# Attention: block mask carried as rows of the second rotary product

## The chip, the cores and the metric

The kernel runs on one core of one Trainium2 chip. The metric is the device time of one execution in microseconds (us); the median of three runs of the kernel before is 1014.16 us (1014.09 to 1014.38).

## What is computed

One residual block of a streaming encoder over 512 frames of width 1024: a half-step SwiGLU layer (ffn1), a token mixer, and a second half-step SwiGLU layer (ffn2), each behind an RMSNorm that is scaled and shifted by vectors computed from a condition c. The mixer has two groups of four heads: a gated DeltaNet, which needs the inverse of a triangular matrix per chunk of 64 frames, and a multi-head latent attention. The change lies in the scores of the attention:

```python
def _rope(x, cos, sin):
    x1, x2 = jnp.split(x, 2, axis=-1)
    return jnp.concatenate([x1 * cos - x2 * sin, x2 * cos + x1 * sin], axis=-1)
...
CHUNK = 64
Q_BLOCK = 128
MLA_NOPE = 128
MLA_ROPE = 64
```

A score is the product of a query and a key over 192 channels: 128 without position ("nope") and 64 rotated by `_rope`; the rotated key is shared by the four heads. The mask is causal by chunks of 64 frames: a query sees every key of its own chunk and of earlier ones. In a block of 128 queries only one corner is masked, the first 64 queries against the last 64 keys of the same block.

## The kernel before, in words

**Stages.** ffn1 runs to about 350 us (the sums for the modulation vectors, L828 on VectorE, run in the same time), the mixer from about 350 to 610 us, ffn2 to the end. Nearly all of TensorE's work is dense products against streamed weights: in the mixer the projection `w_in`, each 128x512 tile as three products of high and low parts (L475, L476, L477). Weights come through tiles `wr` (loaded by SyncE's queue, L139), are cast on ScalarE to `wh` (L234), and VectorE subtracts for the low part `wl` (L235).

**The order.** The mixer's parts are generators: one stream of dense products, and beside it the DeltaNet and the attention in small steps. A scheduler then fixes one order of instructions per engine, so each engine's order is set before the program runs and may change wherever an instruction is added or removed. Every transfer that the steps below name goes through the one queue of SyncE, in order.

**The attention.** `turn_q` (L2070) transposes the rotated queries of two heads at a time; of each head 64 partitions of the tile `qrT` (its own side) take the high part (ScalarE, L2086) and the other 64 the low part (VectorE, L2088). `prep_k` (L2097) transposes the rotated key (`kro`, which holds it twice), and splits it (L2124, with VectorE's subtraction at L1440) into `krh` and `krl`, each holding the key's high or low part on both halves of the partitions. `attend` (L2143) computes the scores of one block of queries and one head, 16 times in all: the nope product in full precision (two passes, L2155), `krh` and `krl` against `qrT` (L2157), and a product of 64 columns in bf16 that adds -1e30 to the masked corner (L2158, from the constant `am` of L1372 to L1376). VectorE takes the maximum (L2160, L2162), ScalarE the exponential (L207), TensorE transposes the result (L2169), ScalarE copies it as `pT` (L2171), and TensorE multiplies it by the values (L2175).

**The inverse.** `delta_a` (L1715) multiplies the DeltaNet keys of each head with themselves (L1712), VectorE scales the result to the tile `at` (L1444), and 16 transfers write it to `a_d` in DRAM. `base_blocks` (L1735) loads it as `ba` (L1746) and VectorE inverts small blocks in a recursion of 15 steps, each a product `bw` (L1444) and a sum `bt` (L1760), which depend on one another; the result goes through DRAM (`t_d`, L1764) to the tile `t` (L1766). `inverse` (L1782) scales it (L1444), multiplies it with `at` in 32x32 tiles (L1806), and goes on from VectorE's `Y` with L1815 and later levels (L1841, L1853, L1877).

Of the kernel before, what the change touches and what calls it, by code (L numbers as in the profile page):

```python
# [11 lines left out]
F32 = mybir.dt.float32  # L12
F32R = mybir.dt.float32r
BF16 = mybir.dt.bfloat16
I32 = mybir.dt.int32
AF = mybir.ActivationFunctionType
ALU = mybir.AluOpType
AX = mybir.AxisListType

P = 128  # L20
NT = 512
D = 1024
KT = D // P
NB = NT // P
# [75 lines left out]
class Block:  # L100
# [1246 lines left out]
    def masks(self):  # L1347
        nc = self.nc
        tile = self.slot(s="mk")
        room = iter([tile[:, i * P:(i + 1) * P] for i in range(4)])  # L1350
        g = nc.gpsimd
        half = next(room).bitcast(BF16)
        self.eye, self.emask = half[:, :P], half[:, P:]
        nc.vector.tensor_copy(self.eye, self.ident)
        g.memset(self.emask, 0.0)
        g.affine_select(out=self.emask, in_=self.emask, pattern=[[1, P]], compare_op=ALU.is_ge, fill=-1.0e30, base=0,
                        channel_multiplier=-1)
        self.triu = next(room)
        g.affine_select(out=self.triu, in_=self.ones, pattern=[[1, P]], compare_op=ALU.is_ge, fill=0.0, base=0,
                        channel_multiplier=-1)  # L1360
        room = next(room)
        by16, self.halves, self.quads, self.lmask = room[:, :8], room[:, 8:10], room[:, 12:16], room[:, 32:64]
        g.affine_select(out=by16, in_=self.ones[:, :8], pattern=[[-16, 8]], compare_op=ALU.is_ge, fill=0.0, base=0,
                        channel_multiplier=1)
        g.affine_select(out=by16, in_=by16, pattern=[[16, 8]], compare_op=ALU.is_ge, fill=0.0, base=15,
                        channel_multiplier=-1)
        nc.vector.tensor_reduce(out=self.halves, in_=by16.rearrange("p (j e) -> p e j", e=2), axis=AX.X, op=ALU.add)
        nc.vector.tensor_reduce(out=self.quads, in_=by16.rearrange("p (j e) -> p j e", e=2), axis=AX.X, op=ALU.add)
        g.memset(self.lmask[:, 16:], 0.0)
        nc.vector.tensor_copy(self.lmask[:, :16], self.halves[:, 1:2].to_broadcast([P, 16]))  # L1370

        am = self.const([P, 192], BF16, s="am")  # L1372
        g.memset(am, 0.0)
        g.memset(am[0:1, 0:64], 1.0)
        g.memset(am[0:1, 128:192], -1.0e30)
        self.amask = am[:, :P], am[:, P:]  # L1376
        sel = self.slot(F32R, s="sel")
        g.memset(sel.bitcast(F32), 0.0)
        self.sel = sel.rearrange("p (h c) -> p h c", h=4)
        for o in (0, 32):  # L1380
            nc.vector.tensor_copy(self.sel[o:o + 4], self.ident[o:o + 4, o:o + 4].unsqueeze(2).to_broadcast([4, 4, P]))
# [692 lines left out]
    def turn_q(self, q):  # L2074

        nc = self.nc
        qr = self.qr
        for g in range(2):
            pt = self.aux()
            for b in range(NB):  # L2080
                nc.tensor.transpose(pt[:, b * P:(b + 1) * P], qr[b][:, g * P:(g + 1) * P], self.ident)

            sides = (slice(0, 64), slice(64, P))
            ts = [self.slot(F32R, "qrT") for _ in sides]
            for t, own in zip(ts, sides):
                nc.scalar.copy(t[own, :], pt[own, :])  # L2086
            for t, own, other in zip(ts, sides, sides[::-1]):
                nc.vector.tensor_tensor(out=t[other, :], in0=pt[own, :], in1=t[own, :].bitcast(F32), op=ALU.subtract)  # L2088
            self.qrT += ts
            yield  # L2090
        for h in range(4):
            c = (h % 2) * 192
            self.qnT.append(self.head_tiles([q[b][h // 2][:, c:c + P] for b in range(NB)], self.gqn))
            yield

    def prep_k(self, kn, q):

        nc = self.nc
        kr = self.kab[:, :288].rearrange("p (b c) -> p b c", b=NB)[:, :, :64]
        s = self.slot(s="krq")  # L2100
# [20 lines left out]
        pt = self.aux()  # L2121
        for b in range(NB):
            nc.tensor.transpose(pt[:, b * P:(b + 1) * P], ko[:, b * P:(b + 1) * P], self.ident)
        self.krT = self.split(pt, "kr")  # L2124
        jk = self.vcol["qkn_k_nope"]
        for h in range(4):
            self.knT.append(self.head_tiles([kn[b][:, h * P:(h + 1) * P] for b in range(NB)], self.cwT[:, jk:jk + 1]))
# [15 lines left out]
    def attend(self, i, h, v, late):  # L2143


        nc = self.nc
# [6 lines left out]
            self.al[h] = self.const([P, NB], s="al")  # L2153
        ps = self.aux()
        nc.tensor.matmul(ps[:, :n], self.qnT[h][:, ts], self.knT[h][:, :n], start=True, stop=False)  # L2155
        for e, kr in enumerate(self.krT):
            nc.tensor.matmul(ps[:, :n], self.qrT[h][:, ts], kr[:, :n], start=False, stop=False)  # L2157
        nc.tensor.matmul(ps[:, n - 64:n], *self.amask, start=False, stop=True)  # L2158
        m = self.small(1, "mx")
        nc.vector.tensor_reduce(out=m, in_=ps[:, :n], axis=AX.X, op=ALU.max, negate=True)  # L2160
        rq = self.rqn[:, 4 * i + h:4 * i + h + 1]
# [44 lines left out]
    def mixer(self, norms):  # L2206
        nc, tc = self.nc, self.tc
        lat = self.latents(norms)
        self.dp = self.ctx.enter_context(tc.tile_pool(name="dp", bufs=1, space=bass.MemoryType.DRAM))
        sides = chain, deltas, att = Side(), Side(), Side()  # L2210
        self.q = self.kv = None
        chain.add(self.lifts(*lat))
# [19 lines left out]
        self.S = None  # L2232

        def prepared():
            self.qrT, self.qnT, self.knT = [], [], []
            while self.q is None:
                yield
            yield from self.prep_q(self.q)
# [250 lines left out]
```

## Time and profile before

| what | value |
|---|---|
| median of three runs | 1014.16 us |
| the profiled execution | 1014.94 us, its span 1013.2 us |
| TensorE (PE) busy | 1001.6 us, 99% of the span |
| VectorE (DVE), ScalarE (ACT) | 822.0 us (81%), 526.7 us (52%) |
| mean granted clock of TensorE | 0.999 of full speed |
| chain that ended last | PE 86%, DVE 7%, DMA 3% |

The span is the time from the first to the last instruction on the core. A busy engine is one that has an instruction in flight; TensorE's products overlap, so the distance from one product's start to the next one's start says what a product takes, and its own duration does not. PEld is TensorE's loading of the stationary operand, which overlaps the products.

### The profile page before, as it was taken

The numbers are of one execution on the slowest core, as the hardware profiler recorded it, in microseconds if no ns is written. First come the engines' busy times: TensorE is split into PE (matmuls) and PEld (weight loads), VectorE is DVE, ScalarE is ACT, GpSimd is POOL, SyncE is SP. The second block draws the span as 40 slices with busy tenths as digits, with TensorE's granted clock in tenths as the row PEclk, the third lists the DMA queues.
The fourth block names the chain that finished last, engine by engine and source line by source line (L and its number), as shares of the span: only waits on it lengthen the run. The fifth ranks groups of instructions, "written<-read, shape, count | busy, mean of one in ns | idle before, by whom it ended". The sixth has DMA issues, their size and how long they took to land.

```text
span 1013.2 us, 18034 instructions
## 1 busy us (share of the span) xinstructions
PE 1001.6 (99%) x7101; PEld 908.1 (90%) x7101; DVE 822.0 (81%) x1461; ACT 526.7 (52%) x954; POOL 30.6 (3%) x74
## 2 busy tenths in 40 slices
PE   7999999999999999999999999999999999999998
PEld 5788999999887889888888888999999999989898
DVE  4779999887797747788987649789998998799984
ACT  4455555556422225548766455375555555655453
POOL 0000000000200000100001012000000000000000
PEclk9999999999999999999999999999999999999999
DMA  9963564434598825412132121212544443323332
GB/s 318 294 203 104 164 209 134 120 97 128 152 324 277 297 78 151 117 44 62 46 75 54 43 63 42 84 43 76 174 122 150 122 129 105 110 83 91 113 104 63
DMA packets 204034, 130.84 MB, mean 129 GB/s; under 512 B 14497, under 2 KB 188590, under 8 KB 203950
## 3 DMA queue, kind: packets, MB, share of 16 engines
q1 hardware_dynamic: 203950, 129.70, 42.0%
q8 instruction: 55, 0.90, 0.4%
q14 instruction: 29, 0.24, 0.1%
HBM read 127.18 MB, written 2.49 MB: 128 GB/s over the span
## 4 chain that ended last, share of the span: by engine, by line
PE 86%; DVE 7%; DMA 3%; issue 1%; SPq 1%; ACT 1%; POOL 0%; DVEq 0%; ACTq 0%
PE pa L360 17%; PE pa L475 13%; PE pb L360 13%; PE pa L476 12%; PE pa L477 12%; PE pa L1207 4%; DMA ar<-in_w_ada 3%; PE pb L1207 3%; SPq L139 1%; PE pb L2175 1%; PE pb L475 1%; PE pb L477 1%; PE pb L476 1%; PE pb L2155 1%; PE pb L1712 1%
## 5 line engine op out<-in xcount | busy, mean ns | idle before, releaser
L275 DVE TENSOR_TENSOR wl<-wr,wh 128x1024 fp32r<-128x1024 f32 x120 | 145.7, 1219 | 26.4 <-ACT wh L279 25.6
L279 ACT CAST wh<-wr 128x1024 fp32r<-128x1024 f32 x120 | 123.2, 1051 | 35.8 <-DVE wr L275 22.0
L234 ACT CAST wh<-wr 128x1024 fp32r<-128x1024 f32 (+1 forms) x77 | 76.8, 1007 | 117.6 <-PE pa L476 106.2
L475 PE MATMUL pa<-hh,wh 128*128 128x512 f32 (+1 forms) x309 | 119.5, 387 | 0.0
L235 DVE TENSOR_TENSOR wl<-wr,wh 128x1024 fp32r<-128x1024 f32 (+1 forms) x77 | 89.2, 1164 | 34.2 <-ACT wh L234 34.1
L477 PE MATMUL pa<-hh,wl 128*128 128x512 f32 (+1 forms) x309 | 116.3, 376 | 0.0
L476 PE MATMUL pa<-hl,wh 128*128 128x512 f32 (+1 forms) x309 | 116.1, 376 | 0.0
L475 PE MATMUL pa<-ah,wh 128*128 128x512 f32 (+1 forms) x262 | 97.9, 374 | 0.0
L476 PE MATMUL pa<-al,wh 128*128 128x512 f32 (+1 forms) x262 | 97.5, 372 | 0.0
L477 PE MATMUL pa<-ah,wl 128*128 128x512 f32 (+1 forms) x262 | 97.3, 371 | 0.0
L275 DVE TENSOR_TENSOR wr<-wr,wr 128x512 f32<-128x512 f32 x120 | 82.4, 687 | 1.7
L828 DVE SCALAR_TENSOR_TENSOR aa<-ar,sc,aa 128x512 f32<-128x512 f32 x98 | 73.3, 748 | 7.7 <-DMA ar<-in_w_ada 6.1
L360 PE MATMUL pa<-th,wh 128*128 128x256 f32 x264 | 74.8, 283 | 0.5 <-ACT z L365 0.5
L360 PE MATMUL pa<-hh,wh 128*128 128x256 f32 x264 | 74.8, 283 | 0.0
L360 PE MATMUL pa<-th,wl 128*128 128x256 f32 x264 | 74.7, 283 | 0.0
L360 PE MATMUL pa<-tl,wh 128*128 128x256 f32 x264 | 74.7, 283 | 0.0
L360 PE MATMUL pa<-hl,wh 128*128 128x256 f32 x264 | 74.7, 283 | 0.0
L360 PE MATMUL pa<-hh,wl 128*128 128x256 f32 x264 | 74.7, 283 | 0.0
L475 PEld LDWEIGHTS pa<-hh,wh 128*128 128x128 f32 x309 | 58.4, 189 | 11.0 <-issue 2.5
L477 PEld LDWEIGHTS pa<-hh,wl 128*128 128x128 f32 x309 | 58.2, 188 | 10.2
L476 PEld LDWEIGHTS pa<-hl,wh 128*128 128x128 f32 x309 | 58.4, 189 | 8.4
L475 PEld LDWEIGHTS pa<-ah,wh 128*128 128x128 f32 x262 | 49.3, 188 | 10.2 <-ACT wh L234 1.7
(484 smaller groups left out, 2768.1 us busy)
## 6 DMA issues: line engine op xcount, KB each, us to landing
wr<-in_ffn_w_in SPq DMA_DIRECT2D x79, 512.0 KB
ar<-in_w_ada SPq DMA_DIRECT2D x128, 256.0 KB
wr<-in_ffn_w_out SPq DMA_DIRECT2D x32, 512.0 KB
wr<-in_w_in SPq DMA_DIRECT2D x21, 512.0 KB
wr<-in_ffn_w_out SPq DMA_DIRECT2D x16, 384.0 KB
wr<-in_w_out SPq DMA_DIRECT2D x8, 512.0 KB
wr<-in_ffn_w_in SPq DMA_DIRECT2D x8, 384.0 KB
ar<-in_w_ada SPq DMA_DIRECT2D x6, 512.0 KB
```

The costliest lines, as they stand in the source:

```text
L139: return self.nc.sync.dma_start(dst, src)
L234: self.nc.scalar.copy(hi, raw)
L235: self.nc.vector.tensor_tensor(out=lo, in0=raw, in1=hi.bitcast(F32), op=ALU.subtract)
L275: sub = lambda out, x, y: nc.vector.tensor_tensor(out=out, in0=x, in1=y, op=ALU.subtract)
L279: nc.scalar.copy(hi[:, :n], raw[:, :n])
L360: nc.tensor.matmul(z, a[:, j, :], b, start=start and j == 0 and i == 0, stop=j == 3 and i == 2, skip_group_check=not start)
L475: mm(out, wh, xh, start=start, stop=False)
L476: mm(out, wh, xl, start=False, stop=False)
L477: mm(out, wl, xh, start=False, stop=stop)
L828: nc.vector.scalar_tensor_tensor(out=acc, in0=a, scalar=sc, in1=acc, op0=ALU.mult, op1=ALU.add)
L1207: nc.tensor.matmul(z, a[:, j, :], b, start=start and j == 0 and i == 0, stop=j == 3 and i == 2, skip_group_check=not start)
L1712: nc.tensor.matmul(pa[:, ps], kh[:, ps], x[:, ps], start=True, stop=True)
```

## The change

`masks` no longer makes the bf16 constant `am`. It makes two tiles of 64 rows and 512 columns: in one (`qm`) row b is 1 over the first half of the columns of block b, in the other (`km`) row b is -1e30 over the second half. Both are written to DRAM. `turn_q` builds a second query tile per head, `qrm`: its own side is a copy of the high part in `qrT`, the other side holds `qm`. `prep_k` builds a tile `krm` for the even heads (low part of the key on the lower half, `km` on the upper), and overwrites the lower half of `krl` with `km` for the odd heads. All these fills are transfers: 2 to DRAM, 8 for the four `qrm`, 3 for `krm` and `krl`. In `attend` the second rotary product takes `krm` or `krl` against `qrm`: it gives the low part of the key times the high part of the query, plus the mask. The product L2158 and its weight load are gone, 16 times. The product of the two low parts, which was part of the score before, is no longer computed.

```diff
--- before.py
+++ after.py
@@ -1369,11 +1369,21 @@
         g.memset(self.lmask[:, 16:], 0.0)
         nc.vector.tensor_copy(self.lmask[:, :16], self.halves[:, 1:2].to_broadcast([P, 16]))
 
-        am = self.const([P, 192], BF16, s="am")
-        g.memset(am, 0.0)
-        g.memset(am[0:1, 0:64], 1.0)
-        g.memset(am[0:1, 128:192], -1.0e30)
-        self.amask = am[:, :P], am[:, P:]
+        self.dp = self.ctx.enter_context(self.tc.tile_pool(name="dp", bufs=1, space=bass.MemoryType.DRAM))
+        one = self.slot(s="am")[:64]
+        g.memset(one, 0.0)
+        by = lambda t: t.rearrange("p (b c) -> p b c", b=NB)
+        first, second = by(one)[:, :, :64], by(one)[:, :, 64:]
+        nc.vector.tensor_copy(first, self.ident[:64, :NB].unsqueeze(2).to_broadcast([64, NB, 64]))
+        qm, km = self.slot(F32R, "am")[:64], self.slot(F32R, "am")[:64]
+        nc.vector.tensor_copy(qm, one)
+        nc.vector.tensor_scalar(out=by(km)[:, :, 64:], in0=first, scalar1=-1.0e30, scalar2=None, op0=ALU.mult)
+        nc.vector.tensor_copy(by(km)[:, :, :64], second)
+        self.amask = []
+        for m in (qm, km):
+            kept = self.dp.tile([64, NT], F32, tag=self.name("am"), name=self.name("am"))
+            self.load(kept, m.bitcast(F32))
+            self.amask.append(kept)
         sel = self.slot(F32R, s="sel")
         g.memset(sel.bitcast(F32), 0.0)
         self.sel = sel.rearrange("p (h c) -> p h c", h=4)
@@ -2087,6 +2097,11 @@
             for t, own, other in zip(ts, sides, sides[::-1]):
                 nc.vector.tensor_tensor(out=t[other, :], in0=pt[own, :], in1=t[own, :].bitcast(F32), op=ALU.subtract)
             self.qrT += ts
+            for t, own, other in zip(ts, sides, sides[::-1]):
+                both = self.slot(F32R, "qrm")
+                self.load(both[other, :].bitcast(F32), self.amask[0])
+                self.load(both[own, :].bitcast(F32), t[own, :].bitcast(F32))
+                self.qrM.append(both)
             yield
         for h in range(4):
             c = (h % 2) * 192
@@ -2121,7 +2136,12 @@
         pt = self.aux()
         for b in range(NB):
             nc.tensor.transpose(pt[:, b * P:(b + 1) * P], ko[:, b * P:(b + 1) * P], self.ident)
-        self.krT = self.split(pt, "kr")
+        self.krT, low = self.split(pt, "kr")
+        even = self.slot(F32R, "krm")
+        self.load(even[64:].bitcast(F32), self.amask[1])
+        self.load(even[:64].bitcast(F32), low[64:].bitcast(F32))
+        self.load(low[:64].bitcast(F32), self.amask[1])
+        self.krM = even, low
         jk = self.vcol["qkn_k_nope"]
         for h in range(4):
             self.knT.append(self.head_tiles([kn[b][:, h * P:(h + 1) * P] for b in range(NB)], self.cwT[:, jk:jk + 1]))
@@ -2153,9 +2173,8 @@
             self.al[h] = self.const([P, NB], s="al")
         ps = self.aux()
         nc.tensor.matmul(ps[:, :n], self.qnT[h][:, ts], self.knT[h][:, :n], start=True, stop=False)
-        for e, kr in enumerate(self.krT):
-            nc.tensor.matmul(ps[:, :n], self.qrT[h][:, ts], kr[:, :n], start=False, stop=False)
-        nc.tensor.matmul(ps[:, n - 64:n], *self.amask, start=False, stop=True)
+        nc.tensor.matmul(ps[:, :n], self.qrT[h][:, ts], self.krT[:, :n], start=False, stop=False)
+        nc.tensor.matmul(ps[:, :n], self.qrM[h][:, ts], self.krM[h % 2][:, :n], start=False, stop=True)
         m = self.small(1, "mx")
         nc.vector.tensor_reduce(out=m, in_=ps[:, :n], axis=AX.X, op=ALU.max, negate=True)
         rq = self.rqn[:, 4 * i + h:4 * i + h + 1]
@@ -2206,7 +2225,6 @@
     def mixer(self, norms):
         nc, tc = self.nc, self.tc
         lat = self.latents(norms)
-        self.dp = self.ctx.enter_context(tc.tile_pool(name="dp", bufs=1, space=bass.MemoryType.DRAM))
         sides = chain, deltas, att = Side(), Side(), Side()
         self.q = self.kv = None
         chain.add(self.lifts(*lat))
@@ -2232,7 +2250,7 @@
         self.S = None
 
         def prepared():
-            self.qrT, self.qnT, self.knT = [], [], []
+            self.qrT, self.qrM, self.qnT, self.knT = [], [], [], []
             while self.q is None:
                 yield
             yield from self.prep_q(self.q)
```

The scheduler's order changes with it. Three places are shown; lines from L1372 on stand 10 to 19 lines further down in the changed code.

**TensorE, ahead of the DeltaNet's key products (L1712, now L1722).** First before, then with the change; `kro` is the rotated key, `kn` are the nope keys, and L475 to L477 on `pa` are dense products.

```order
L1639 MATMUL pb_5371<-rw_5008,sel_3146 128x512
L1640 LDWEIGHTS mk_3129
L1640 MATMUL pb_5371<-mk_3129 128x512
L2123 MATMUL pb_5380<-ident_85,kro_5191 128x128 x4
L2028 MATMUL pb_5389<-ident_85,kn_4900 128x128
```

```order
L1649 MATMUL pb_5391<-rw_5016,sel_3156 128x512
L1650 LDWEIGHTS mk_3129
L1650 MATMUL pb_5391<-mk_3129 128x512
L477 MATMUL pa_5623<-hh_4090,wl_5536 128x512
L475 MATMUL pa_5698<-hh_4076,wh_5619 128x512
L476 MATMUL pa_5698<-hl_4077,wh_5619 128x512
L477 MATMUL pa_5698<-hh_4076,wl_5620 128x512
L475 MATMUL pa_5698<-hh_4078,wh_5619 128x512
L476 MATMUL pa_5698<-hl_4079,wh_5619 128x512
L2138 MATMUL pb_5400<-ident_85,kro_5199 128x128 x4
L477 MATMUL pa_5698<-hh_4078,wl_5620 128x512
L2038 MATMUL pb_5413<-ident_85,kn_4908 128x128
```

Dense products stand ahead of the key's transposes that stood behind them. Counted over the program, 18 more dense products lie ahead of the transposes of `kro`, and 22 more ahead of the last of the 16 key products (L475 to L477 counted alike); two scores lie ahead of it in both orders.

**VectorE, in the last steps of the recursion (L1760, now L1770).** First before, then with the change; `wl` and `cv` are the dense stream's low part and the DeltaNet's convolution.

```order
L1760 TENSOR_REDUCE bt_5618<-bw_5621 128x13
L235 TENSOR_TENSOR wl_6197<-wr_6194,wh_6196 128x1024
L1444 TENSOR_TENSOR bw_5621<-ba_5615,bt_5618 128x196
L1656 SCALAR_TENSOR_TENSOR cv_5853<-pa_5777,cwT_3774,cv_5853 128x511
L1760 TENSOR_REDUCE bt_5618<-bw_5621 128x14
L1656 SCALAR_TENSOR_TENSOR cv_5853<-pa_5777,cwT_3774,cv_5853 128x510
L1444 TENSOR_TENSOR bw_5621<-ba_5615,bt_5618 128x225
L1656 SCALAR_TENSOR_TENSOR cv_5853<-pa_5777,cwT_3774,cv_5853 128x509
L1760 TENSOR_REDUCE bt_5618<-bw_5621 128x15
```

```order
L1770 TENSOR_REDUCE bt_5640<-bw_5643 128x13
L1454 TENSOR_TENSOR bw_5643<-ba_5637,bt_5640 128x196
L1770 TENSOR_REDUCE bt_5640<-bw_5643 128x14
L1454 TENSOR_TENSOR bw_5643<-ba_5637,bt_5640 128x225
L1770 TENSOR_REDUCE bt_5640<-bw_5643 128x15
L235 TENSOR_TENSOR wl_6406<-wr_6403,wh_6405 128x1024
L1666 SCALAR_TENSOR_TENSOR cv_5950<-pa_5882,cwT_3784,cv_5950 128x511
```

Other work that stood between the steps stands behind the last one. Over all 15 steps the recursion has one L235 and three L1656 fewer between its instructions, and one L2160 with its L2162 more; three more of its instructions follow one another with nothing between.

**TensorE, between the 32x32 products of the inverse (L1806 and L1815, now L1816 and L1825).** The rows up to the second of the two, first before, then with the change; `pr` is the exponential of a score.

```order
L2175 MATMUL pb_6055<-vn_4905,pT_5931 128x128
L2169 MATMUL pb_6059<-ident_85,pr_5893 128x128 x3
L475 MATMUL pa_5948<-hh_4074,wh_5860 128x512
L476 MATMUL pa_5948<-hl_4075,wh_5860 128x512
L477 MATMUL pa_5948<-hh_4074,wl_5861 128x512
L475 MATMUL pa_5948<-hh_4076,wh_5860 128x512
L476 MATMUL pa_5948<-hl_4077,wh_5860 128x512
L477 MATMUL pa_5948<-hh_4076,wl_5861 128x512
L1815 MATMUL pb_6071<-T_5918,Y_6020 32x32 x64
```

```order
L2194 MATMUL pb_6071<-vn_4913,pT_5948 128x128
L2188 MATMUL pb_6075<-ident_85,pr_5910 128x128 x3
L1825 MATMUL pb_6087<-T_5935,Y_6037 32x32 x64
L477 MATMUL pa_5965<-hh_4090,wl_5879 128x512
```

The six dense products between L1806 and L1815 are gone from there: 11 more stand ahead of L1806, 5 more ahead of L1815. Seven scores lie ahead of L1806 in both orders.

SyncE's queue changes at one place that matters beside these. Before, one load of `w_in`, 8 of the 16 dumps of `at`, another load of `w_in` and the other 8 dumps follow one another. With the change the 8 fills of `qrm`, a load of `w_in`, one of `w_out`, and the 3 fills of `krm` and `krl` stand ahead of all 16 dumps.

## Rows read from the trace of the kernel before

**Rows 1.** The page, part 1: busy time, share of the span, instructions.

```profile
PE 1001.6 (99%) x7101; PEld 908.1 (90%) x7101; DVE 822.0 (81%) x1461; ACT 526.7 (52%) x954; POOL 30.6 (3%) x74
```

**Rows 2.** Stretches of 20 us: busy us (count) per engine, clock, DMA share, GB/s.

```profile
540.00:560.00 20.00, 19.54 (x417) 16.27 (x417) 15.36 (x28) 14.69 (x33) 3.53 (x3) 1.00 0.20 57
```

**Rows 3.** Timeline of PE: start us, duration us, line; two dense products 16 apart.

```profile
507.73 0.39 PE L475 MATMUL pa<-hh,wh 128*128 128x512 f32 x1
...
511.39 0.39 PE L476 MATMUL pa<-hl,wh 128*128 128x512 f32 x1
```

**Rows 4.** Timeline of PE: end of a score, its mask, the next products.

```profile
587.00 0.40 PE L2157 MATMUL pb<-krl,qrT 128*128 128x512 f32 x1
587.24 0.20 PE L2158 MATMUL pb<-am 128*128 128x64 bf16 x1
587.28 0.48 PE L475 MATMUL pa<-hh,wh 128*128 128x512 f32 x1
587.59 0.39 PE L476 MATMUL pa<-hl,wh 128*128 128x512 f32 x1
```

**Rows 5.** Timeline of PEld, the same place: the weight loads behind the mask's.

```profile
587.24 0.20 PEld L475 LDWEIGHTS pa<-hh,wh 128*128 128x128 f32 x1
587.36 0.19 PEld L476 LDWEIGHTS pa<-hl,wh 128*128 128x128 f32 x1
```

**Rows 6.** Timeline of DVE: the split key, `at`, the recursion, the loaded `t`.

```profile
500.48 0.69 DVE L1440 TENSOR_TENSOR krl<-pb,krh 128x512 fp32r<-128x512 f32 x1
...
509.17 0.69 DVE L1444 TENSOR_TENSOR at<-pb,ed 128x512 f32<-128x512 f32 x1
...
525.50 0.42 DVE L2160 TENSOR_REDUCE mx<-pb 128x1 f32<-128x256 f32 x1
...
526.88 0.22 DVE L1760 TENSOR_REDUCE bt<-bw 128x8 f32<-128x64 f32 x1
527.14 0.30 DVE L1444 TENSOR_TENSOR bw<-ba,bt 128x81 f32<-128x81 f32 x1
...
530.66 1.22 DVE L235 TENSOR_TENSOR wl<-wr,wh 128x1024 fp32r<-128x1024 f32 x1
531.80 0.49 DVE L1444 TENSOR_TENSOR bw<-ba,bt 128x196 f32<-128x196 f32 x1
532.21 0.74 DVE L1656 SCALAR_TENSOR_TENSOR cv<-pa,cwT,cv 128x511 f32<-128x511 f32 x1
...
534.90 0.38 DVE L1760 TENSOR_REDUCE bt<-bw 128x15 f32<-128x225 f32 x1
...
540.82 0.69 DVE L1444 TENSOR_TENSOR t<-t,mk 128x512 f32<-128x512 f32 x1 [0.45 <-DMA t<-t_d]
```

**Rows 7.** Timeline of PE: first score, and around L1806 and L1815.

```profile
503.42 0.28 PE L2157 MATMUL pb<-krl,qrT 128*128 128x128 f32 x1
...
541.28 0.40 PE L477 MATMUL pa<-hh,wl 128*128 128x512 f32 x1
541.65 1.28 PE L1806 MATMUL pb<-t,at 32*32 32x32 f32 x128
...
545.25 0.49 PE L2169 MATMUL pb<-ident,pr 128*128 128x128 f32 x3
...
546.73 0.39 PE L477 MATMUL pa<-hh,wl 128*128 128x512 f32 x1
547.04 1.29 PE L1815 MATMUL pb<-T,Y 32*32 32x32 f32 x128
...
549.43 0.94 PE L2175 MATMUL pb<-vn,pT 128*128 128x128 f32 x6 [0.47 <-ACT pT L2171]
```

**Rows 8.** Timeline of SyncE's queue: the last eight dumps, the load of `t`.

```profile
508.50 3.63 SPq L139 DMA_DIRECT2D a_d<-at  x8
...
538.02 0.37 SPq L1766 DMA_DIRECT2D t<-t_d  x1
```

**Rows 9.** Waits of SyncE's queue from 486 to 545 us: total, times, longest.

```profile
SPq L139 <- DVE wl L235: 31.4, 6, 11.1
```

## The prediction

> **What bounds the kernel.** I read the busy shares first: TensorE is busy 99% of the span [rows 1], so time leaves where TensorE has less to do, and comes where it must wait. The stretches of 20 us come next: nearly all are full, and the one from 540 to 560 us, where the attention runs beside the inverse of the DeltaNet, shows 19.54 of 20 us at a clock of 1.00 [rows 2]. The timeline of TensorE says what stands there. A dense product costs 0.229 us, start to start: 16 steps in 3.66 us [rows 3]. Before the first 32x32 product, L1806, 0.37 us pass from the dense product ahead, where 0.31 pass ahead of L1815, which is not late [rows 7]: so L1806 waits 0.06 us for the tile `t` and stands at the edge. Whatever makes `t` later than TensorE's own place in its work becomes idle time. That is the second thing to look at, beside the products saved.
>
> **The mask products, minus 2.0 us.** Two starts are misleading: the mask's product and the next one are drawn 0.04 us apart. But the second product behind the mask starts 0.59 us after the second rotary product [rows 4], where two dense steps take 0.46 [rows 3]: 0.13 for the mask. The weight loads say why: the load of the product behind the mask begins when the mask's product does, and the load after that begins 0.12 later [rows 5], as that product starts. 64 columns are too short to cover a weight load. So 0.125 times 16 scores is 2.0 us; bounds 16 times 0.04 = 0.6 and 16 times 0.13 = 2.1. I take 2.0, since the weight loads and the distances agree. [...]
>
> **The dense products that move.** The last key product of the DeltaNet comes 22 dense products later and two masks earlier: 22 times 0.229 less 0.25 is +4.8 us [rows 3]. VectorE makes the last `at` 509.17 us in [rows 6]; it follows the second score and the key products behind it, so it moves with them by 4.8. Then comes the chain of dumps, load, recursion, `t_d` and `t`. Its transfers stay as they are. In the recursion one L235 (1.14 from its start to the next) and three L1656 (0.66 each) leave, 3.1 us in all, and a maximum of 0.42 with its small product, some 0.45 together, joins [rows 6]. Three steps more stand bare: a bare one leaves 0.04 us before the next (526.88 plus 0.22, then 527.14), where a covered one overlaps by some 0.08 (530.66 plus 1.22, then 531.80) [rows 6]; 3 times 0.12 is 0.36. The recursion is 2.3 us shorter, so `t` comes 4.8 - 2.3 = 2.5 us later. TensorE reaches L1806 after 11 more dense products and 7 masks fewer: 2.5 - 0.9 = +1.6 us. What is left, **0.85 us, is a new wait at L1806**. Bounds: nothing, if the recursion were 3.1 us shorter and the masks dearer or `at` less bound to the scores; 3.2, if it were not shorter at all.
>
> **Behind L1806.** The six dense products between L1806 and L1815, 1.4 us, are gone. L1815 itself needs `Y`, which VectorE has longer to make with fewer rows ahead of it, so I cost that at nothing. The value products are nearer: before, the one at 549.43 waits 0.47 us for ScalarE's copy `pT`, 4.2 us after the transposes at 545.25 [rows 7]. With the change L1815 and five dense products instead of six lie in that stretch, so the wait grows by one dense product, 0.23, and the next copies are no earlier. I take +0.35. Bounds: -0.47, the wait gone because ScalarE has caught up during the wait at L1806; +1.4, all the cover of the six missing.
>
> **The 13 transfers.** The two dumps of mask rows lie among ffn1's loads, some 250 us before use. The other eleven cost the queue about 0.45 us each to issue (3.63 over 8 [rows 8]), 5 us, while it would wait for `at` anyway; the 8 fills of `qrm` are issued right behind the `qrT` they copy, well ahead of the first score. The tile `krm` is at the edge. `krl` is made at 500.48 plus 0.69 [rows 6], and its transposes stand 18 dense products later, +4.1: 505.3. Issue at 0.45 and a landing as of `t`, 2.8 (538.02 [rows 8] to 540.82 [rows 6]), gives 508.5. The first product that reads it stood at 503.42 [rows 7], moves by 4.8 and has one L1649 ahead of it now: 508.5. I take +0.15, bounds 0 and 0.8. The four small VectorE operations of the mask tiles replace none on the path and fall in ffn1, where VectorE is not the bound; nothing. Its cover gone, they would cost under 0.7 each [rows 6].
>
> **The sum.** -2.0 + 0.85 + 0.35 + 0.15 = -0.65 us. Against the profiled execution, 1014.94 us (span 1013.2 and 1.74 around it), that is 1014.3; this execution lies 0.78 above the median of 1014.16, so the median comes to 1013.5. Differences of over 0.2%, 2.03 us, are what a measurement of this kernel can tell from none.
>
> **Rivals.**
> - *No new wait.* VectorE's last `at` may not follow the scores by the full 4.8 us (its row is 2 us behind the key products), and then `t` is in time. Then the 2.0 stand alone, 1012.1 us, on the edge of faster; with the 0.47 us of the old wait gone too, 1011.7. For it: the recursion has less in its way. Against: the wait of 0.06 already there. 0.17.
> - *The mask was cheap.* If the load behind a mask is covered and only the drawn 0.04 us a mask falls, 0.6 us is saved and 1.45 added [rows 4]: 1015.0 us. [...] Against it stand the weight loads at 0.12 us [rows 5]. 0.12.
> - *The recursion does not gain.* The work that leaves it runs in its gaps anyway; the wait at L1806 becomes 3.2 in place of 0.85, 2.3 more: 1015.9 us, still within 0.2%. 0.08.
> - *The queue holds the dumps* (slower). With the change a load of `w_in` and one of `w_out` stand ahead of all 16 dumps, and each waits until VectorE's L235 has freed a weight buffer: 31.4 us over 6 waits, 5.2 each, up to 11.1 [rows 9]. If the second is freed after the last `at` is made, every us beyond it goes into `a_d`, `t` and L1806 one for one. One mean wait, 5.2, gives 1013.5 + 5.2 = 1018.7; it is slower by more than can be told apart from 2.7 us on. Against it: the queue is held back by less, since `at` is itself 4.8 us later and VectorE's L235 stand earlier in its order. 0.08.
>
> **Chances.** My forecast gets 0.55. Faster by over 0.2%: half of the first rival and a little of the forecast's lower edge, 0.13. Slower by over 0.2%: the last rival and a small part of the third, 0.09. The rest, 0.78, within 0.2%. The range reaches from 1011.9 (no new wait, lower half left out) to 1016.2 (the recursion does not gain, and `krm` is late by its bound): it leaves out the queue's rival and part of the first.
>
> **What would show it.** Right: the second product behind a score 0.13 us nearer; the last `at` near 514 us, `t` near 543.3; idle time before L1806 of about 0.9 us; the wait for `pT` behind L1815 still there; TensorE's busy time down by some 2 us. Wrong: no idle time at L1806 with a time near 1012; or dumps of `at` issued well after `at`; or a first `krm` product with idle time of over 0.8 us before it; or a wait in ffn1 behind the two dumps, where I put nothing.

## The result, and the profile after

| | kernel before | with the change |
|---|---|---|
| median of 6 runs | 1014.27 us (1012.75 to 1016.77) | 1018.74 us (1017.67 to 1021.03) |
| ratio, 95% interval | | 1.0047 (1.0036 to 1.0058) |
| profiled execution, its span | 1014.94 us, 1013.2 us | 1018.37 us, 1016.7 us |

The change is slower by 0.47%, some 4.8 us, where the prediction had 0.65 us faster. The time is 2.5 us above the range. Of the six executions of the change, the three with a mean granted clock of 1.000, the profiled one among them, took 1017.67 to 1018.37 us, and the three with 0.997 or 0.998 took 1019.11 to 1021.03 us. The page of the profile after, part 1, answers to [rows 1]: TensorE has 16 products fewer and is busy 1.4 us longer.

```profile
PE 1003.0 (99%) x7085; PEld 908.7 (89%) x7085; DVE 821.9 (81%) x1465; ACT 526.5 (52%) x954; POOL 30.2 (3%) x72
```

**One place is the mixer.** The stretch of [rows 2] after (busy us and count per engine, clock, DMA share, GB/s) shows TensorE busy 17.23 us of 20 where before had 19.54:

```profile
540.00:560.00 20.00, 17.23 (x397) 14.16 (x396) 14.68 (x27) 12.86 (x27) 3.01 (x3) 1.00 0.27 67
```

The timeline of TensorE there (start, duration, line; in brackets the idle time ahead and what ended it). L1806 and L1815 of before are L1816 and L1825 now, so this answers to [rows 7]:

```profile
544.88 0.48 PE L476 MATMUL pa<-hl,wh 128*128 128x512 f32 x1
547.78 1.28 PE L1816 MATMUL pb<-t,at 32*32 32x32 f32 x128 [2.42 <-DVE t L1454]
...
551.71 1.29 PE L1825 MATMUL pb<-T,Y 32*32 32x32 f32 x128
552.93 0.50 PE L477 MATMUL pa<-hh,wl 128*128 128x512 f32 x1
553.78 0.49 PE L2175 MATMUL pb<-nT,nT 128*128 128x128 f32 x2 [0.35 <-ACT pr L207]
...
563.35 0.49 PE L2194 MATMUL pb<-vn,pT 128*128 128x128 f32 x2 [0.23 <-ACT pT L2190]
```

L1806 waits 2.42 us for `t`. VectorE and SyncE's queue after show what makes `t` late (they answer to [rows 6] and [rows 8]):

```profile
516.09 0.69 DVE L1454 TENSOR_TENSOR at<-pb,ed 128x512 f32<-128x512 f32 x1
...
526.01 0.69 DVE L1454 TENSOR_TENSOR qk<-pb,ed 128x512 f32<-128x512 f32 x1 [1.08 <-PE pb L2175]
526.62 0.15 DVE L1454 TENSOR_TENSOR bw<-ba,bt 128x1 f32<-128x1 f32 x1
...
540.10 0.39 DVE L1770 TENSOR_REDUCE bt<-bw 128x15 f32<-128x225 f32 x1
...
546.94 0.69 DVE L1454 TENSOR_TENSOR t<-t,mk 128x512 f32<-128x512 f32 x1 [1.90 <-DMA t<-t_d]
```

```profile
509.45 10.92 SPq L139 DMA_DIRECT2D a_d<-at  x16
521.53 1.35 SPq L1756 DMA_DIRECT2D ba<-a_d  x2
...
541.76 0.59 SPq L139 DMA_DIRECT2D wr<-in_w_out  x1
543.27 0.38 SPq L1776 DMA_DIRECT2D t<-t_d  x1
```

All positions here include a shift of 1.54 us that was there before the mixer began. Less that, the last `at` comes 5.38 us later (516.09 against 509.17), the recursion's first step 6.26 (526.62; before it stood at 518.82), its last sum 3.66, and `t` 4.58.

**The other place is the start.** The same product, L885's first in the modulation vectors, in the profile before and after:

```profile
192.38 1.07 PE L885 MATMUL pb<-aa,ones 128*32 128x512 f32 x8
```

```profile
193.92 1.06 PE L885 MATMUL pb<-aa,ones 128*32 128x512 f32 x8
```

And the first 50 us, before and after:

```profile
0.00:50.00 50.00, 43.98 (x278) 33.14 (x279) 30.58 (x59) 22.21 (x38) 2.35 (x12) 1.00 0.95 307
```

```profile
0.00:50.00 50.00, 43.85 (x256) 32.62 (x257) 29.48 (x58) 22.18 (x38) 1.92 (x9) 1.00 1.00 298
```

The DMA engines are busy all the time (share 1.00 for 0.95) and move less (298 GB/s for 307). In this stretch the change runs nothing new; what differs is where things lie. The dropped constant `am` was 384 bytes in each partition, and the tiles allocated behind it, those of the loads among them, stand 384 bytes lower: by the programs' addresses at multiples of 512 bytes before, and 128 above one now.

In this pair of profiles the gap goes from 1.54 us at 192 us to 3.46 at the end; the mixer costs 1.9.

### The profile page after: what moved, and what is told of

Its sections match the earlier page's. It is cut to its first block, busy times and chain, and to the rows that moved or that the text cites. A ratio compares the mean times of both kernels' runs of the same rounds, so it can differ in the third digit from the quotient of the medians.

```text
span 1016.7 us, 18031 instructions
## 1 busy us (share of the span) xinstructions
PE 1003.0 (99%) x7085; PEld 908.7 (89%) x7085; DVE 821.9 (81%) x1465; ACT 526.5 (52%) x954; POOL 30.2 (3%) x72
## 4 chain that ended last, share of the span: by engine, by line
PE 86%; issue 5%; DVE 3%; DMA 3%; SPq 1%; ACT 1%; POOL 0%; DVEq 0%; ACTq 0%; POOLq 0%
PE pa L360 18%; PE pb L360 13%; PE pa L475 13%; PE pa L477 12%; PE pa L476 12%; PE pa L1207 4%; PE pb L1207 3%; SPq L139 1%; DMA ar<-in_w_ada 1%; DMA wr<-in_ffn_w_in 1%; PE pb L475 1%; PE pb L476 1%; PE pb L477 1%; PE pb L2175 1%; PE pb L2194 1%
## 5 line engine op out<-in xcount | busy, mean ns | idle before, releaser
L475 PE MATMUL pa<-hh,wh 128*128 128x512 f32 (+1 forms) x309 | 118.5, 383 | 0.0
L477 PE MATMUL pa<-hh,wl 128*128 128x512 f32 (+1 forms) x309 | 116.6, 377 | 0.0
L235 DVE TENSOR_TENSOR wl<-wr,wh 128x1024 fp32r<-128x1024 f32 (+1 forms) x77 | 89.2, 1164 | 28.4 <-ACT wh L234 28.2
L475 PE MATMUL pa<-ah,wh 128*128 128x512 f32 (+1 forms) x262 | 97.9, 374 | 0.0
L477 PE MATMUL pa<-ah,wl 128*128 128x512 f32 (+1 forms) x262 | 97.3, 371 | 0.0
L475 PEld LDWEIGHTS pa<-hh,wh 128*128 128x128 f32 x309 | 58.3, 189 | 11.4 <-issue 2.5
L477 PEld LDWEIGHTS pa<-hh,wl 128*128 128x128 f32 x309 | 58.2, 188 | 10.0
L475 PEld LDWEIGHTS pa<-ah,wh 128*128 128x128 f32 x262 | 49.3, 188 | 10.0 <-ACT wh L234 1.7
```

The source lines that it names most:

```text
L235: self.nc.vector.tensor_tensor(out=lo, in0=raw, in1=hi.bitcast(F32), op=ALU.subtract)
L475: mm(out, wh, xh, start=start, stop=False)
L477: mm(out, wl, xh, start=False, stop=stop)
```

## Experiments: the start

**a_pad** keeps the dropped constant's place, unused:

```diff
+        pad = self.const([P, 192], BF16, s="am")
         one = self.slot(s="am")[:64]
```

> The changed kernel with the dropped constant tile (384 bytes a partition) kept, unused, so that every later tile stands at its address of before. The changed kernel measured 4.5 us slower, but its trace shows only 1.9 us of that in the mixer; the rest stood before 50 us, where the loads of the first layer arrive. Theory layout: the start comes back, 1016.2, ratio near 1.002. Theory scatter (or the DRAM tiles): as the changed kernel, ratio 1.0035 to 1.0055, and its mixer loses 1.9 us in the trace again.

1015.65 us, ratio 1.0017 (1.0009 to 1.0026). Of the 4.8 us, 3.0 are gone (1.0047 less 1.0017) with the same instructions besides three small fills of the unused place.

**b_128** and **b_256** move the same tiles in the kernel before, by 128 and by 256 bytes (256 columns as below, and 320):

```diff
-        am = self.const([P, 192], BF16, s="am")
+        am = self.const([P, 256], BF16, s="am")
```

> The kernel before with its bf16 constant widened from 192 to 256 columns: 128 bytes more in each partition, nothing else. Theory of the layout: tiles that the loads fill then stand at 128 bytes past a multiple of 512, as in the change, and loads become slower where they bound the start; the first 50 us show a DMA share of 0.99 to 1.02 at about 300 GB/s in place of 0.95 at 310, TensorE is 1.5 to 2.8 us later from 192 us on, and the time is 1015.5 to 1017 (ratio 1.0015 to 1.003). Rival (the start's shift scatters, or belongs to other edits of the change): the same as before, ratio 0.9995 to 1.0005.

> The kernel before with its bf16 constant widened from 192 to 320 columns: 256 bytes more in each partition, so that the tiles behind it stand at 256 bytes past a multiple of 512 (128 past in the change and in b_128). If what counts is a multiple of 512, the loads of the start are slow as in b_128 (DMA share about 1.0 at about 300 GB/s in the first 50 us) and the time is 1015 to 1016.5; if a multiple of 256 does, it is as before, ratio 0.9995 to 1.0005, and the share 0.95.

b_128: 1015.71 us, 1.0019 (1.0010 to 1.0028). b_256: 1013.90 us, 1.0003 (0.9994 to 1.0012). Their first 50 us, b_128 and then b_256:

```profile
0.00:50.00 50.00, 44.09 (x261) 32.88 (x261) 30.52 (x59) 22.44 (x38) 2.40 (x12) 1.00 1.02 303
```

```profile
0.00:50.00 50.00, 43.88 (x280) 32.94 (x281) 30.50 (x59) 22.59 (x39) 2.45 (x12) 1.00 0.95 308
```

Of the places tried, 128 bytes past a multiple of 512 cost 1.9 us (b_128) and 256 bytes past one cost nothing (b_256, ratio 1.0003): of the two multiples that the expectation names, these runs fit 256 bytes and not 512. All 17 profiles fall apart the same way: in the twelve whose tiles stand at a multiple of 256 the share over the first 50 us is 0.95 or 0.96, in the five at 128 past one it is 0.99 to 1.02. The product L885 shown above starts at 191.1 us on average in the twelve (189.62 to 192.84) and at 193.3 in the five (192.49 to 193.92), 2.2 us later. Why the loads of the start are slower at 128 past is not shown.

**b_again**, the kernel before once more, says what repeats.

> The kernel before, unchanged, as a measure of scatter. In the profile of the changed kernel 1.5 us of the loss arise within the first 50 us, where both kernels issue the same instructions. Theory scatter: this run's first dense products and its landmark at 51 us (the last statistics product) move against the first profile of before by one or two us too, and its time differs from before by up to 1 us. Theory layout (the constant that the change drops, or the DRAM tiles it adds, shift addresses and slow the first loads): this run repeats the first profile's start to within 0.3 us, and the ratio to before is 1.000.

1013.65 us, ratio 0.9999 (0.9990 to 1.0008). In its profile the steps of the mixer stand where the first profile has them, to 0.07 us (the recursion's first step to 0.21), beside a shift of 0.46 that is there from 192 us on; this is more than the 0.3 that the layout theory allowed. The profiled execution, 1017.48 us, is 2.1 us longer still behind TensorE's last product. So single profiles scatter in the start, by 3.2 us among the twelve above, and at the end, and the mixer can be compared to some 0.2 us.

## Experiments: what a mask product was worth

**n1_no_mask** is the kernel before without the mask's product (no corner is masked):

```diff
-        nc.tensor.matmul(ps[:, n - 64:n], *self.amask, start=False, stop=True)
```

> Before without the 16 mask products and without any mask (the corner is left unmasked). The order of instructions hardly moves (one dense product more ahead of the key products of the inverse), and there is no new transfer. If a mask product costs 0.125 us, the time falls by 2.0 us (ratio 0.9980); if it costs the drawn 0.04 us, by 0.6 us (ratio 0.9994). No new idle time ahead of the first 32x32 product beyond about 0.5 us.

1013.85 us, 1.0001 (0.9992 to 1.0009): nothing. The trace says where it went.

```profile
542.94 1.28 PE L1806 MATMUL pb<-t,at 32*32 32x32 f32 x128 [2.12 <-DVE t L1444]
```

From the first score to the sixth, ahead of which both orders have the same dense products, TensorE gains 0.52 us on before over five masks, 0.10 each (503.42 to 525.14 before, 503.01 to 524.21 here). From the tenth to the sixteenth it gains 0.66 over six, 0.11 each, or 0.14 without a wait of 0.19 us at 570.61 that before does not have. Between them L1806 waits 2.12 us: the saved time is handed over to `t`, and more, because a load of `w_out` now goes out right behind the loads of `ba` (515.77 where before had 517.45) and the first step of the recursion waits 1.64 us for them. Two things follow: the mask was worth about what the rows said, and before `t` nothing that TensorE saves is kept.

**n7_dumps** is the kernel before with the mask's tiles built and dumped as in the change, and not used.

> Before with the two mask tiles built and written to DRAM as in the change, unused; scores, operands and mask product as before. Theory that the 13 transfers cost only in the mixer: the same time as before within 0.5 us. Theory that the dumps or the DRAM tiles slow the loads of the first layer: 1.5 us or more longer, and the loss stands before 350 us in its trace.

1013.77 us, 0.9999 (0.9990 to 1.0007). The four VectorE operations and two dumps in ffn1 cost nothing that can be told apart, as predicted.

## Experiments: the wait for `t`

**n8_engine_fills** and **n3_pool_fills** have no transfers of mask rows and no dumps. In n8 GpSimd writes the mask rows early, ScalarE copies the high part, and VectorE subtracts straight into `krm` and `krl`; in n3 GpSimd makes all fills where the change has its transfers. Both lack the constant's place, as the change does. In outline (n8, then n3):

```diff
-                self.load(both[other, :].bitcast(F32), self.amask[0])
-                self.load(both[own, :].bitcast(F32), t[own, :].bitcast(F32))
+            nc.scalar.copy(self.qrM[2 * g + h][own, :], pt[own, :])
...
+                self.mask_rows(both, other, False, nc.gpsimd)
+                nc.gpsimd.tensor_copy(both[own, :], t[own, :])
```

> The change with no transfer: mask rows written by GpSimd ahead of the query transposes, the copies of the high part by ScalarE, the low parts of the key by two subtractions of VectorE. TensorE's order stays that of the change within two dense products (20 more ahead of the key products, 11 more ahead of the first 32x32 product). Theory order (the late key products make the chain late): the wait at the first 32x32 product stays near 2 us and the mixer loses 1.5 to 2 us in the trace. Theory queue (the 11 fills and the dumps behind them make it late): the wait shrinks to under 1 us and the mixer loses under 0.7.

> The change with all 13 transfers gone: mask rows and copies are written by GpSimd straight into the operand tiles. The key products of the inverse come 10 dense products later than before (22 in the change), the first 32x32 product 3 earlier (11 later in the change). Theory that the transfers cause the loss: the mask products' 2.0 us come back and the new wait at the first 32x32 product is about 0.4 to 1 us: 1012.9 to 1013.4. Theory that the operand swap itself loses: near the changed kernel, 1018.

n8: 1019.33 us, 1.0051 (1.0037 to 1.0064). It keeps the change's order of TensorE to within two dense products, L1806 waits 2.24 us, and it is as slow with no fill in SyncE's queue. Its loads of `ba` go out 1.63 us earlier than the change's (521.53), and yet the recursion begins only 0.39 earlier (526.62), behind a `qk` that waits for a score, as in the change:

```profile
519.90 1.34 SPq L1742 DMA_DIRECT2D ba<-a_d  x2
```

```profile
525.62 0.69 DVE L1440 TENSOR_TENSOR qk<-pb,ed 128x512 f32<-128x512 f32 x1 [1.06 <-PE pb L2174]
526.23 0.15 DVE L1440 TENSOR_TENSOR bw<-ba,bt 128x1 f32<-128x1 f32 x1
```

So the fills are not the cause, and it is not the dumps in the queue that make the recursion begin late; what n8 shares with the change is TensorE's order. n3, whose order differs, waits less: 1016.16 us, 1.0024 (1.0015 to 1.0034). Its key products are 10 dense products later than before instead of 22, and L1806 waits 0.72 us.

**bt_free** and **at_free** take the chain away from `t`: it is loaded from the dumped mask rows, so that the DeltaNet's result is left out, while the recursion and its dump still run (before with n7's dumps, and a_pad; the line is at_free's).

```diff
-        nc.sync.dma_start(self.t16, t_d.rearrange("q i s c -> (i s) q c"))
+        nc.sync.dma_start(self.t16, self.amask[0].rearrange("r (e q c) -> (r e) q c", e=2, q=16))
```

> The kernel before, with the mask's tiles made and dumped but unused, and with the tile t loaded from those dumps in place of the recursion's result, so that L1806 does not wait for the recursion (the recursion and its dump still run; the DeltaNet's result is left out by it). The control for at_free. Both theories: before had only 0.06 us of wait at L1806, so the time stays at ratio 0.9985 to 1.0005.

> The change with its dropped constant's place kept (as a_pad, 1015.65 us), and with t loaded from the dumped mask rows in place of the recursion's result (the DeltaNet's result is left out by it; the recursion still runs). The scheduler then puts L1806 at nearly the same dense product as in its control, 1544 against 1542. Theory of the chain (key products 22 dense products later make t late; the masks are worth 0.10 to 0.125 each): no wait at L1806, no drop of the clock behind it, and 1.2 to 2.0 us less than the control: 1011.8 to 1012.9. Rival one (the masks were worth only 0.04 each): 0.2 to 0.7 less than the control, about 1013.3. Rival two (other waits of the new order eat the gain: the first score, pT, Y): no less than the control, 1013.7 to 1015.5.

bt_free: 1014.57 us, 1.0005 (0.9996 to 1.0014). at_free: 1013.26 us, 0.9991 (0.9982 to 1.0000). TensorE in at_free, L1806 and the value products behind:

```profile
538.79 1.40 PE L1820 MATMUL pb<-t,at 32*32 32x32 f32 x128
...
548.06 0.94 PE L2198 MATMUL pb<-vn,pT 128*128 128x128 f32 x6 [1.03 <-ACT pT L2194]
```

With no wait for `t` the change is 1.4 us faster than its control (0.9991 less 1.0005), and 2.6 faster than a_pad with the wait (1.0017 less 0.9991). The 1.4 lies in the chain theory's 1.2 to 2.0, with some 1.3 to either side by the intervals. The time itself lies above the theory's 1012.9 and beside the first rival's 1013.3, so this pair alone does not part the two. L1806 stands behind 1544 dense products in at_free and 1542 in bt_free, 15 fewer than in the change and 6 fewer than before. So this is not a_pad with the wait alone removed, and the control has only a part of that shift.

**m1_late_fills** and **m2_more_cover** do the change's full work, with the constant's place kept, and alter mainly the cover: the dense products between the last key product and L1806 (89 before, 78 in the change, 91 and 110 here). In m1 `turn_q` issues the eight fills of `qrm` behind its last head; m2 has this too, issues the three of `krm` and `krl` at the end of `prep_k`, and steps the chain at 1.1 in place of 1 for a dense step.

```diff
-            for t, own, other in zip(ts, sides, sides[::-1]):
-                both = self.slot(F32R, "qrm")
...
             self.qnT.append(self.head_tiles([q[b][h // 2][:, c:c + P] for b in range(NB)], self.gqn))
             yield
+        sides = (slice(0, 64), slice(64, P))
+        for h, t in enumerate(self.qrT):
+            own, other = sides[h % 2], sides[1 - h % 2]
+            both = self.slot(F32R, "qrm")
...
```

> The change with the dropped constant's place kept, and the eight fills of qrm issued at the end of turn_q in place of behind each pair of heads; the same work otherwise. The scheduler then leaves the transposes of the rotated key where before had them; key products 17 dense products later than before (22 in the change), L1806 19 later (11), 91 dense products between the two as against 78 in the change and 89 before. Theory of the chain: 13 dense products more of cover, 3.0 us, take away the 2.4 us of idle time at L1806 and the clock's drop behind it, and with the start in place the time is 1012.0 to 1013.4 (ratio 0.998 to 0.9995). Rival (dense products now missing behind L1806, 6 and 7 ahead of L1841 and L1853 where before had 12 and 12, turn into waits there for Y, 1 to 2 us): 1013.5 to 1015.5, with idle time at L1815 or L1841 in the place of L1806's.

> As m1_late_fills, and the fills of krm and krl at the end of prep_k, with the chain's steps 1.1 to a dense step in place of 1 while the key products run: key products 17 dense products later than before, 110 between the last of them and L1806 (89 before, 78 in the change). Theory of the chain: no idle time at L1806 at all; what it is worth beyond m1 is nothing, since that wait is gone there already. Rival: L1806 so late that the later levels (L1841 to L1877: 11, 3 and 12 dense products apart) wait for VectorE in its place: 1014 to 1017 us.

m1: 1014.19 us, 1.0009 (1.0000 to 1.0018). m2: 1013.41 us, 0.9995 (0.9987 to 1.0004). In m1 L1806 has no wait, as expected, but its rival came true as well, at another instruction: 2.2 us of idle time for ScalarE's `pT` behind it.

```profile
552.04 0.94 PE L2198 MATMUL pb<-vn,pT 128*128 128x128 f32 x6 [1.24 <-ACT pT L2194]
...
559.90 0.49 PE L2198 MATMUL pb<-vn,pT 128*128 128x128 f32 x2 [0.96 <-ACT pT L2194]
```

m2 has neither of the two, and still 1.39 us at L1806. It has the most cover, but its chain begins late: in its order the first `krm` products stand 6.9 us behind the first `krh` product (511.09 and 504.19), a maximum on VectorE waits 3.61 us for them, and the last `at` behind it comes at 515.87 (511.24 in m1). Two loads of `w_out` stand ahead of the last eight dumps of `at` in its queue, but the first of the eight goes out at 514.00, as soon as its `at` is made (513.29 and 0.68 of work). `t` lands 3.41 us after its issue.

```profile
548.15 1.29 PE L1818 MATMUL pb<-t,at 32*32 32x32 f32 x128 [1.39 <-DVE t L1456]
```

```profile
511.35 0.62 DVE L2183 TENSOR_REDUCE mx<-pb 128x1 f32<-128x128 f32 x2 [3.61 <-PE pb L2181]
```

So m1 does the change's work 0.8 us faster than a_pad and m2 2.2 (from 1.0017 to 1.0009 and 0.9995); m1's interval overlaps a_pad's, m2's does not. m2 is no slower than before; neither is faster than before by what can be told apart.

**n3_padded**, a try at a version that beats both, failed:

```diff
+        pad = self.const([P, 192], BF16, s="am")
-        self.dense_units(4, Rates(sides, (1, 0, 1.5)), 1, conv_done(0, qT))
+        self.dense_units(4, Rates(sides, (1, 0, 1.75)), 1, conv_done(0, qT))
```

> A try at a version that beats both: the change with the fills of qrm, krm and krl made by GpSimd in place of transfers and from no dumps, the dropped constant's place kept, and the attention's steps 1.75 to a dense step in place of 1.5 while the key products run: key products 9 dense products later than before (22 in the change), L1806 two later (11), so 1.6 us less cover than before and 3.6 us less work that the recursion shares VectorE with. Theory of chain and layout: no idle time, or under 1 us, at L1806, the start as before, and the time 1012.3 to 1013.8 (ratio 0.998 to 0.9995). Rival (waits elsewhere eat the gain): 1014 to 1015.5.

1016.89 us, 1.0031 (1.0021 to 1.0040). L1806 waits only 0.49 us and the start is as before, but the rate moved work at the mixer's end, where a new wait of 2.07 us stands at 601 us for the attention's normalised output (`on`). A rate moves everything behind it, so it can't test one wait.

**a_chain_early** and **b_chain_early** step the chain at 1.5 in place of 1, in the change and in before.

> The change with the same rate of 1.5; 113 dense products stand between the key products and the first 32x32 product (78 in the change). Theory that the chain takes the gain: no wait at the first 32x32 product, so that the 16 mask products' 1.6 to 2.0 us show: 1.0 to 2.0 us faster than before with the same rate, and some 4 us faster than the change. Theory that the operand swap costs in other ways (fills, queue): no faster than before with the same rate.

> Before with the steps of the inverse's chain issued at a rate of 1.5 instead of 1 beside the query columns of the projection, so that 99 dense products stand between the key products and the first 32x32 product instead of 89. A control for the next run: if the wait for t (0.06 us) and the wait for pT (0.47) are all that TensorE loses in the mixer, it gains at most 0.5 us, 1013.6; a loss of up to 2 us if the steps behind it get in each other's way.

1017.74 us (1.0040, 1.0027 to 1.0052) and 1020.72 us (1.0072, 1.0059 to 1.0084). The change is 1.0 us faster than at its own rate, where 4 was expected, and has no wait at L1806 (113 dense products of cover). Before is 7 us slower, where at most 2 was expected: it idles 3.26 us ahead of the last of L1815's products, where a_chain_early idles 1.57 (550.72), and the granted clock is 0.50 from 546 to 548 us, where two dense products stand 0.43 us apart (547.03 to 547.46) and not 0.229.

```profile
544.40 0.22 PE L1815 MATMUL pb<-T,Y 32*32 32x32 f32 x2 [3.26 <-issue]
```

What ends that wait is not marked, and why it comes was not followed up. The 3.2 us between the two are more than 16 masks are worth, so this pair does not show what the change's product saves.

## Why the prediction was wrong, point by point

- **The dropped constant**: not costed at all. The sum has no term for it, and the start was taken as unchanged. It measured +1.9 (b_128) to +3.0 us (a_pad), and 2.2 by the seventeen profiles: the largest part of the error.
- **"0.85 us is a new wait at L1806"**: the right mechanism at the right place, too small. It is 2.42 us. The mis-sized step is "2.5 us later" for `t`, which came 4.58 later. Of the 2.1 us between, the last `at` gives 0.6 (5.38 for 4.8). The recursion begins another 0.88 us later (6.26 less 5.38), behind a `qk` that waits 1.08 us for a score, a wait that the sum did not have. And "its transfers stay as they are" fails for `t`: it lands 3.67 us after its issue (543.27 to 546.94) where before needed 2.80, with a 512 KB load of `w_out` issued 1.5 us ahead of it. The recursion was foreseen well, 2.6 us shorter for 2.3. The error lay inside the bound: 3.2 us "if it were not shorter at all". A lower clock behind the wait, which the last section shows for a_pad (0.50) and n8 (0.50), had no term.
- **TensorE's own place at L1806, +1.6**: about 2.2 (4.58 less the 2.4 us that it waits); TensorE was held up on the way too.
- **The mask products, minus 2.0**: right in size, rather too large. Behind a score of 512 columns the second dense product stands 0.45 and 0.47 us on (570.66 to 571.11, 590.58 to 591.05), 0.59 before [rows 4]. But the sum took that row for all 16, and behind scores of 128 columns the distance falls by 0.08 only (0.47 behind the one at 570.09 before, 0.39 behind 573.89). n1's trace gives 0.10 to 0.14 each, 1.6 to 2.2 in all. The rival of the cheap mask falls; the 1.45 us that it adds are 0.10 more than the waits of the sum (0.85, 0.35 and 0.15), without a reason given.
- **Behind L1806, +0.35**: the wait for `pT` behind L1815 is gone; in its place 0.35 us for `pr` at 553.78 and 0.23 for `pT` at 563.35 stand: 0.58 in place of 0.47, so 0.11 more, less than forecast and inside the bounds.
- **The 13 transfers, +0.15**: no cost of a transfer shows: n7's dumps change nothing (0.9999), and n8, with none of the 13, is no faster (1.0051 for 1.0047). Ahead of the first score TensorE loses about 0.5 us (its shift is 7.07 at that place: 1.54 from the start, 5.04 for 22 dense products), and the waits there are not marked with a releaser, so whose they are stays open.
- **The slower rival, "the queue holds the dumps"**: its price gave 1018.7 us, by chance the measured time. In the change the two loads go out at 502.98 and 504.20, well ahead of the last `at`, and no weight load stands among the dumps; they end 3.6 us after the last `at` (520.37 against 516.78; before 2.3), and n8 has the same time with no fills. It fell. In m2 two such loads do stand ahead of the last eight dumps, and they too are out before the `at` that those wait for.
- **The range**: its upper end, 1016.2, is not the sum of what it names; 1015.9 and 0.65 more for `krm` make 1016.5. The time lies above both.

Taken apart by the ratios, the 4.8 us are +3.0 from the place in memory (the change less a_pad), +2.6 with the chain in `t` (a_pad less at_free: the idle time, the lower clock behind it and the shift of 15 dense products), and -0.9 for the rest, the masks among it (at_free less before). They make up the whole by the way they are formed; each has an interval of 0.9 to 1.4 us to either side.

## What to carry to other kernels

A constant that is dropped moves everything allocated behind it: look at the addresses of the tiles that loads fill, and try the kernel with the old place kept, before a difference of 0.2% is put down to the code that changed; here 128 bytes were worth 1.9 us (b_128), 256 nothing (b_256), and the place kept 3.0 us (a_pad). Where an engine that is 99% busy stands at the edge of a long chain of small steps through other engines and DRAM, time saved ahead of that point was not kept here (n1 waits 2.12 us at L1806), and what the chain lost beyond the engine's own delay was paid as idle time (2.42 us in the change); cost each landing in that chain as an open term, not as "unchanged" (that of `t` took 3.67 us for 2.80). An order that a scheduler makes anew can have other waits elsewhere (2.2 us at `pT` in m1, 2.07 us at `on` in n3_padded), so test the wait with a version that takes the dependence away and a control with the same edit.

## What the runs showed that was not expected

In two profiles, a_pad's and n8's, the clock falls behind the wait at L1806, beside the idle time. In a_pad TensorE idles 2.48 us there (540 to 544 us); then the granted clock of the next stretches is 0.78, 0.50 and 0.87, and the score behind runs at that clock: its nope product takes 1.79 us where the change's profile has 1.13 at a clock of 1.00.

```profile
540.00:542.00 2.00, 1.08 (x9) 0.76 (x7) 0.71 (x2) 1.97 (x4) 0.00 (x0) 1.00 1.03 187
542.00:544.00 2.00, 0.44 (x51) 0.47 (x54) 1.17 (x2) 2.00 (x5) 0.00 (x0) 1.00 0.03 3
544.00:546.00 2.00, 2.00 (x102) 1.36 (x89) 1.49 (x3) 1.68 (x3) 0.00 (x0) 0.78 0.04 8
546.00:548.00 2.00, 2.00 (x7) 1.35 (x6) 0.55 (x1) 0.00 (x0) 0.00 (x0) 0.50 0.00 0
548.00:550.00 2.00, 2.00 (x109) 1.83 (x109) 0.30 (x2) 1.58 (x2) 0.00 (x0) 0.87 0.00 0
```

```profile
543.56 1.28 PE L1820 MATMUL pb<-t,at 32*32 32x32 f32 x128 [2.48 <-DVE t L1458]
544.77 1.79 PE L2179 MATMUL pb<-nT,nT 128*128 128x512 f32 x2
...
549.15 1.29 PE L1829 MATMUL pb<-T,Y 32*32 32x32 f32 x128
```

n8 shows the same (0.93, 0.50 and 0.71 from 546 to 552 us). The change's own profile does not: after 2.42 us of idle time its clock stays at 1.00. From L1806 to L1815 a_pad needs 5.59 us (543.56 to 549.15) and the change 3.93 (547.78 to 551.71), so the low clock costs 1.66 us. The three longer executions of the change, with mean clocks of 0.997 and 0.998, would fit such a fall; but no trace shows them, and b_again's profile has 0.998 without a fall in the mixer, so this is not shown. Why one profile falls and the other doesn't is open.
